# A transformer block with sparse and dense experts: reshaped gates, no end stage, U products beside the gates

## The chip, the cores and the metric

The kernel runs on one core of a Trainium2 chip. The metric is device time in microseconds (us), median of three runs. A profiled execution, taken separately, gives the rows below.

## The reference

One block over 1024 tokens of width 1024, float32. A mixing part (RMS norm, w_in, a pooling mixer and a gated mixer, w_out, residual) gives h. Then the PEER feed-forward, and a last RMS norm:

```python
q = (xb @ wq).reshape(T, 8, 2, 128)                   # 8 heads, 2 halves
s = einsum('thpd,phkd->thpk', q, keys)                # 16 lists of 128 scores
s_top, i_top = top_k(s, 16)
cand = s_top[:, :, 0, :, None] + s_top[:, :, 1, None, :]
best_s, best_pos = top_k(cand.reshape(T, 8, 256), 16) # 16 of 16384 experts per head
gate = softmax(best_s)
act = gelu(einsum('td,thkd->thk', xb, u_tab[idx]))
out = einsum('thk,thkd->td', gate * act, v_tab[idx])
```

## The kernel before

Tokens are eight blocks of 128. They pass the mixing part in three groups: first (blocks 0, 1), middle (2 to 5), last (6, 7). The feed-forward is done in two ways.

**Sparse blocks (0, 1, 6, 7).** For each of a token's 128 experts GpSimd (POOL) gathers one U row per token, 512 KB for a block of 128 tokens (`gather`, L475), and VectorE (DVE) takes the dot product (L501). `sparse_v` (L513) gathers V rows, four tokens at a time; ScalarE (ACT) sets the weights into a zero-padded tile `wz` (L520), and TensorE (PE) sums with 16 matmul instructions per step (L531), 32 steps per block. Parts are named U0, V0, U1 and so on; `sparse` (L665) hands them out in phases: EARLY before the dense loop, LATE beside it, with 32 rows (AFTER) kept back. `behind` (L487) ties the U0 and V0 matmuls to marks in PE's order.

**Dense blocks (2 to 5), 512 tokens.** All 16384 experts are computed. Expert (a, b) is row a of column b; there are 128 columns. First the gates are spread into a table G[expert, token] in DRAM (`gates_dense`, L554): for four tokens at a time (a step; TB = 4, 128 steps in all) DVE compares the token's 128 first and second keys with a row of numbers (`oh`, L567, L569), gate values are multiplied in by ACT for two tokens (L579) and by DVE for two (L581), PE multiplies the two one-hot sets (L582), and ACT copies the result from the accumulator to `gs` (two copies, L585); 32 tokens fill two half tiles, which go out (L589). `scale` (L592) normalises the middle group's rows, held in `sd`, into a high and a low part `xdh`, `xdl`. Then `dense` (L604): for every column c it loads U and V (L628, L633), splits both, computes U's product by 24 matmuls (`mu`, L642), gelu (L644), times the gates read from G (`gc`, L639; L645), splits that, and every three columns `down` (L615) multiplies by V (24 matmuls a column, `mm`, L619) and adds into `hD` (L623). `finish` (L545) does the last norm and the output.

**Selection.** `score` (L340) makes the lists' scores and calls `top16` (L368, five DVE operations) on each; `pick` (L380) selects 16 of the candidate sums for a block, `turn` (L462) transposes the result.

**Order.** Python generators set the trace order: `weave` (L695) takes so many steps of the gates per step of the last group's mixing, residual and score (L784 to L788); the rest of the gates follows (L798), then selection of blocks 6 and 7 (L800), scaling, EARLY, and the dense loop with LATE beside it (L817). A scheduler fills gaps on each engine with later instructions that are ready, so instructions can run ahead of this order. After the loop an end stage opens 16 row buffers (`rowe`) and does the last 32 rows of V7 (L822). Loads and stores are issued by SP's queue, gathers by POOL's.

Of the kernel before, what the change touches and what calls it, by code (L numbers as in the profile page):

```python
# [17 lines left out]
P = 128  # L18
# [8 lines left out]
PH = 8  # L27
# [20 lines left out]
GS = 3  # L48
# [18 lines left out]
def hybrid_block(ctx: ExitStack, tc: tile.TileContext, t: dict, out: bass.AP):  # L67
# [40 lines left out]
    gS = dram.tile([S, D], F32, name="gS")  # L108

# [193 lines left out]
    def residual(fc, fr, chunks, most):  # L303
# [6 lines left out]
        for q in range(4):  # L310
            cols = slice(q * WC, (q + 1) * WC)
            for ch, p in zip(chunks, project(fr, "w_out", q * WC, [ch.a for ch in chunks], True)):
                nc.vector.tensor_add(ch.h[:, :, cols], ch.h[:, :, cols], p)

                def quarter(ch=ch, q=q, cols=cols):
                    hg = tmp(fr, 2 * WC).rearrange("p (k e) -> p k e", e=WC)
                    nc.vector.tensor_mul(hg, ch.h[:, :, cols], g2row[:, None, cols].to_broadcast([P, NB, WC]))
                    if not d0 <= ch.t0 // P < d0 + DBLK:
                        nc.sync.dma_start(gS[ch.t0:ch.t0 + N, cols].rearrange("(k p) e -> p k e", p=P), hg)
# [4 lines left out]
                    nc.scalar.activation(ch.s[:, 2 * q:2 * q + 2, :], p, AF.Copy)  # L324
# [15 lines left out]
    def score(fr, tk, chunks):  # L340

        for ch in chunks:
            for k in range(NB):
# [15 lines left out]
        for q in range(NLIST // 2):  # L359
# [6 lines left out]
            yield  # L366

# [37 lines left out]
    def pick_heads(tk, top, tix, n, keys, gate_kh):  # L405
# [46 lines left out]
        for i in range(2):  # L452
            eq = tk.tile([P, TK, TK, PH], BF16, name="eq", tag="eq", bufs=1)[:, :, :, :n]
# [59 lines left out]
    def sparse_v(b):  # L513
# [4 lines left out]
        for j in range(32):  # L518
            z = wz[j % 2]
# [34 lines left out]
    def gates_dense(gp, b):  # L554
# [4 lines left out]
        for part in range(P // GT):  # L559
            kb = (b - d0) * (P // GT) + part  # L560
            gs = [gp.tile([P, NK // 2, GT], F32, name="gs", bufs=GS) for _ in range(2)]
            for t0 in range(0, GT, TB):

                oh = gp.tile([P, 2 * TB, NK], F32, name="oh", bufs=OH)
                tok = part * GT + t0
                half = TB // 2
                nc.vector.tensor_tensor(oh[:, 0:TB, :], iota_k[:, None, :].to_broadcast([P, TB, NK]),  # L567
                                        iT[:, 0, tok:tok + TB, None].to_broadcast([P, TB, NK]), op=ALU.is_equal)
                nc.vector.tensor_tensor(oh[:, TB:TB + half, :], iota_k[:, None, :].to_broadcast([P, half, NK]),  # L569
                                        iT[:, 1, tok:tok + half, None].to_broadcast([P, half, NK]), op=ALU.is_equal)  # L570
                if t0 // TB % 2:
                    p = ps1.tile([P, TB, NK], F32, name="mu", bufs=2)
                else:
                    p = ps.tile([P, TB, NK], F32, name="mm")
                for i in range(TB):
                    at = slice(tok + i, tok + i + 1)
                    c = oh[:, TB + i, :]
                    if i < half:
                        nc.scalar.activation(c, c, AF.Copy, scale=iT[:, 2, at])  # L579
                    else:  # L580
                        nc.vector.tensor_scalar(c, iota_k, iT[:, 1, at], iT[:, 2, at], op0=ALU.is_equal, op1=ALU.mult)  # L581
# [5 lines left out]
            for i, g in enumerate(gs):  # L587
                n = NK // GI // 2
                nc.sync.dma_start(G[i * n:(i + 1) * n, kb].rearrange("a i b t -> i a (b t)"),  # L589
                                  g.rearrange("i (a b) t -> i a (b t)", b=GI))  # L590

    def scale(tk, xdh, xdl):  # L592

        both = tk.tile([P, 2, ND], F32, name="both", tag="eq", bufs=1)
        r2B, x = both[:, 0, :], both[:, 1, :]
# [4 lines left out]
        for c in range(NDC):  # L600
            nc.vector.tensor_mul(x, sd[:, c, :], r2B)
            split(xdh[:, c, :], xdl[:, c, :], x)

    def dense(de, xdh, xdl):  # L604

        v_rows = t["peer_v"].rearrange("(a b) d -> b a d", b=NK)
        xd = [(xdh[:, c, :], xdl[:, c, :]) for c in range(NDC)]
        with tc.tile_pool(name="da", bufs=2, side="right", reuse_waits="tile") as da:
# [17 lines left out]
            for c in range(NK):  # L626
                raw = de.tile([P, NDC, P], F32, name="raw_u", tag="raw", bufs=3)
                nc.sync.dma_start(raw, t["uT"][c])  # L628
                uh = de.tile([P, NDC, P], F32R, name="uh")
                ul = de.tile([P, NDC, P], F32R, name="ul")  # L630
                split(uh, ul, raw)
# [9 lines left out]
                p = ps1.tile([P, ND], F32, name="mu", bufs=2)  # L641
                mm3(p, [(uh[:, i, :], ul[:, i, :]) for i in range(NDC)], xd)  # L642
                a = de.tile([P, ND], F32, name="a", bufs=2)
                nc.scalar.activation(a, p, AF.Gelu_apprx_tanh)  # L644
                nc.vector.tensor_mul(a.rearrange("i (k t) -> i k t", t=GT), a.rearrange("i (k t) -> i k t", t=GT), gc[:, :, c % GI, :])  # L645
                wh = da.tile([P, ND], F32R, name="wh", bufs=GROUP + 1)
# [3 lines left out]
                if c == 1:  # L650
                    load()
# [215 lines left out]
```

## Time and profile before

| what | us |
|---|---|
| median of 3 runs (lowest, highest) | 2702.26 (2700.18, 2703.74) |
| the profiled execution's own time | 2707.89 |
| its span, first to last instruction | 2705.8 |
| PE busy / DVE / ACT / POOL in the span | 2438.1 / 1896.4 / 774.3 / 1198.3 |
| moved by DMA | 831.49 MB, mean 307 GB/s |

Busy time is a union per engine. PE's matmuls overlap in a row's durations, so rates are read from their starts. PEld is PE's weight load. The granted clock (PEclk) is a share of full speed; PE has two levels, 1.2 and 2.4 GHz. A wait is put down to what ended it last.

### The profile page before, as it was taken

To read this page: it belongs to the slowest core of one execution; us is meant where nothing else is said; L and a number is where in the kernel's file an instruction comes from. 1 tells how busy PE (TensorE), PEld (TensorE's weight loads), DVE (VectorE), ACT (ScalarE), POOL (GpSimd) and SP (SyncE) were. 2 spreads that over 40 slices of the span, in tenths; PEclk is the share of its full clock that TensorE was granted. 3 is DMA by queue.
4 is the path that set the end of the run, shared out by engine and by line. 5 is a ranking of instruction groups with operands and counts; after the bars stand their busy time and mean duration, and the time that the engine had idled before them with its cause. 6 is when DMAs were issued, how large, how long until landed. Compare 5 with 4: busy or idle time off the path is not lost.

```text
span 2705.8 us, 34765 instructions
## 1 busy us (share of the span) xinstructions
PE 2438.1 (90%) x11968; PEld 1862.7 (69%) x11968; DVE 1896.4 (70%) x4643; ACT 774.3 (29%) x1424; POOL 1198.3 (44%) x1098
## 2 busy tenths in 40 slices
PE   7997899888866467999999999999999999999993
PEld 6886788767645144777777777777777777766770
DVE  2389979987797977986776767666676766433451
ACT  3220011245635252222222222322222222222220
POOL 0034753143443544655555555465455555344004
PEclk9998999999978689999999999999999999999996
DMA  7677998599988799999999999899999999889317
GB/s 250 210 245 230 384 344 284 168 313 315 333 286 296 255 307 348 361 356 324 365 354 342 341 339 364 328 361 375 327 342 359 349 348 331 324 329 359 119 39 287
DMA packets 345392, 831.49 MB, mean 307 GB/s; under 512 B 25216, under 2 KB 158848, under 8 KB 345216
## 3 DMA queue, kind: packets, MB, share of 16 engines
q0 software_dynamic: 147456, 536.94, 54.0%
q1 hardware_dynamic: 197760, 292.33, 31.4%
q8 instruction: 95, 1.56, 0.2%
q14 instruction: 81, 0.66, 0.1%
HBM read 785.13 MB, written 44.04 MB: 306 GB/s over the span
## 4 chain that ended last, share of the span: by engine, by line
PE 67%; DVE 15%; DMA 9%; issue 5%; ACT 2%; POOL 1%; SPq 0%; POOLq 0%; ACTq 0%; DVEq 0%
PE mm L176 8%; PE mm L139 8%; PE mm L140 8%; PE mu L141 8%; PE mm L141 8%; PE mu L139 8%; PE mu L140 8%; PE po L531 8%; DVE junk L501 3%; DMA G<-gs 2%; DMA rowt<-peer_v,idxT 2%; DVE rest L372 1%; PE mm L582 1%; DMA w<-w_out 1%; PE mu L582 1%
## 5 line engine op out<-in xcount | busy, mean ns | idle before, releaser
L480 POOL DMA_INDIRECT rowt<-peer_v,idxT x432 | 500.5, 1159 | 709.0 <-PE po L531 501.6
L480 POOL DMA_INDIRECT rowv<-peer_u,idx x288 | 353.6, 1228 | 176.4 <-DVE junk L501 105.7
L480 POOL DMA_INDIRECT rowt<-peer_u,idx x224 | 261.4, 1167 | 346.5 <-DVE top L370 166.4
L139 PE MATMUL mm<-vh,wh 128*128 128x512 f32 x1024 | 400.8, 395 | 14.4 <-ACT wh L131 8.4
L141 PE MATMUL mu<-xdh,ul 128*128 128x512 f32 x1024 | 403.0, 394 | 6.6 <-DVE ul L132 6.6
L139 PE MATMUL mu<-xdh,uh 128*128 128x512 f32 x1024 | 401.2, 393 | 6.2 <-ACT xdh L131 3.7
L140 PE MATMUL mu<-xdl,uh 128*128 128x512 f32 x1024 | 401.8, 392 | 1.2 <-DVE xdl L132 0.7
L140 PE MATMUL mm<-vl,wh 128*128 128x512 f32 x1024 | 401.0, 392 | 0.1
L501 DVE SCALAR_TENSOR_TENSOR junk<-rowv,h 128x1024 bf16<-128x1024 f32 x288 | 352.0, 1222 | 44.2 <-DMA rowv<-peer_u,idx 41.2
L141 PE MATMUL mm<-vh,wl 128*128 128x512 f32 x1024 | 376.9, 392 | 0.0
L623 DVE TENSOR_TENSOR hD<-hD,mm 128x512 f32<-128x512 f32 x344 | 225.8, 682 | 184.4 <-PE mm L141 183.5
L501 DVE SCALAR_TENSOR_TENSOR junk<-rowt,h 128x1024 bf16<-128x1024 f32 x224 | 271.9, 1214 | 19.6 <-DMA rowt<-peer_u,idx 18.2
L531 PE MATMUL po<-rowt,wz 128*32 128x512 f32 x1728 | 237.8, 650 | 38.0 <-DMA rowt<-peer_v,idxT 38.0
L139 PEld LDWEIGHTS mm<-vh,wh 128*128 128x128 f32 x1024 | 193.0, 189 | 75.1 <-issue 14.2
L141 PEld LDWEIGHTS mu<-xdh,ul 128*128 128x128 f32 x1024 | 192.6, 188 | 65.8 <-DVE ul L132 9.4
L139 PEld LDWEIGHTS mu<-xdh,uh 128*128 128x128 f32 x1024 | 192.1, 188 | 58.7 <-issue 9.2
L140 PEld LDWEIGHTS mu<-xdl,uh 128*128 128x128 f32 x1024 | 192.8, 188 | 53.8 <-issue 9.2
L141 PEld LDWEIGHTS mm<-vh,wl 128*128 128x128 f32 x1024 | 192.6, 189 | 50.1 <-issue 9.2
L140 PEld LDWEIGHTS mm<-vl,wh 128*128 128x128 f32 x1024 | 193.2, 189 | 42.4 <-issue 2.5
L644 ACT ACTIVATE a<-mu 128x512 f32<-128x512 f32 x128 | 76.0, 594 | 491.2 <-PE mu L141 490.0
L132 DVE SCALAR_TENSOR_TENSOR ul<-raw_u,uh 128x1024 fp32r<-128x1024 f32 x128 | 156.2, 1220 | 78.3 <-ACT uh L131 78.3
L131 ACT ACTIVATE vh<-raw_v 128x1024 fp32r<-128x1024 f32 x128 | 131.0, 1052 | 235.8 <-PE mm L141 216.9
(167 smaller groups left out, 3374.3 us busy)
## 6 DMA issues: line engine op xcount, KB each, us to landing
raw_u<-uT SPq DMA_DIRECT2D x128, 512.0 KB, 6.9
raw_v<-peer_v SPq DMA_DIRECT2D x128, 512.0 KB, 7.2
G<-gs SPq DMA_DIRECT2D x32, 1024.0 KB, 14.8
w<-wq SPq DMA_DIRECT2D x48, 512.0 KB, 6.6
w<-w_in SPq DMA_DIRECT2D x36, 512.0 KB, 4.8
w<-w_out SPq DMA_DIRECT2D x24, 512.0 KB, 6.6
h<-x SPq DMA_DIRECT2D x16, 512.0 KB, 7.7
rowt<-peer_v,idxT POOLq DMA_INDIRECT x432
```

Source lines behind the costliest of these rows:

```text
L131: nc.scalar.activation(hi, src, AF.Copy)
L132: nc.vector.scalar_tensor_tensor(lo, src, 1.0, f32(hi), op0=ALU.mult, op1=ALU.subtract)
L139: nc.tensor.matmul(dst, lh, rh, start=first and c == 0, stop=False)
L140: nc.tensor.matmul(dst, lh, rl, start=False, stop=False)
L141: nc.tensor.matmul(dst, ll, rh, start=False, stop=last and c == n - 1)
L176: mm = nc.tensor.matmul(dst[:, i, :], lhs, rhs, start=c == 0, stop=c == NDC - 1)
L480: ins = nc.gpsimd.indirect_dma_start(out=rowt, out_offset=None, in_=t[table], in_offset=bass.IndirectOffsetOnAxis(ap=ids, axis=0))
L501: nc.vector.scalar_tensor_tensor(junk, r, 1.0, h, op0=ALU.mult, op1=ALU.mult, accum_out=act[:, j:j + 1])
L531: mm = nc.tensor.matmul(po[g * 32:(g + 1) * 32, q * HALF:(q + 1) * HALF], z[:, g, 31 - j:63 - j], r[:, q * HALF:(q + 1) * HALF], start=j = ...
L582: mm = nc.tensor.matmul(p[:, i, :], oh[:, i, :], c, start=True, stop=True)
L623: nc.vector.tensor_add(hq, hq, p)
L644: nc.scalar.activation(a, p, AF.Gelu_apprx_tanh)
```

## The change

The gate step compares both keys of four tokens in one operation, ACT alone multiplies the gate values in, the matmuls of one step write interleaved (token innermost), and one copy empties the accumulator into one tile of 128 rows. The middle group's rows go to DRAM (`sS`) instead of `sd`; `scale` reads them back, two chunks at a time, and stands ahead of the rest of the gates. The U products of the first AHEAD = 7 columns (`up`) are handed out over the last 46 gate steps and kept in `ua`. The last group's scores go to DRAM (`cS`); `lists` reads them and makes the top-16 lists behind the gates, just ahead of the selection of blocks 6 and 7. V0 is split: 64 rows EARLY, 64 LATE. The loop hands out all 768 LATE rows by column 125, in proportion to U and V products done; the end stage is gone. Until seven columns are done the loop's gathers use the old row buffers alone. Four `wz` tiles take the place of two; `wh` and `wl` have three buffers instead of four, `sc` three instead of four; the final norm's row loads inside the loop.

```diff
-ROWS, VROWS, EROWS = 7, 4, 16
+AHEAD = 7
+ROWS, VROWS = 7, 4
-EARLY = ({"U0": 128}, {"V0": 128, "U1": 64})
-LATE = ({"U1": 64}, {"V1": 128, "U6": 128}, {"V6": 128, "U7": 128}, {"V7": 128})
-AFTER = 32
+EARLY = ({"U0": 128}, {"V0": 64, "U1": 64})
+LATE = ({"V0": 64, "U1": 64}, {"V1": 128, "U6": 128}, {"V6": 128, "U7": 128}, {"V7": 128})
...
-    for i in range(2):
+    for i in range(4):
         z = const.tile([P, 4, 63], F32, name=f"wz{i}")
...
-                    nc.scalar.activation(ch.s[:, 2 * q:2 * q + 2, :], p, AF.Copy)
+                    sq = ch.s[:, 2 * q:2 * q + 2, :]
+                    nc.scalar.activation(sq, p, AF.Copy)
+                    if D0 <= ch.t0 < D0 + ND:
+                        nc.sync.dma_start(sS[2 * q:2 * q + 2, :, ch.t0 - D0:ch.t0 - D0 + N]
+                                          .rearrange("c p s -> p c s"), sq)
...
-                sc = tk.tile([P, 2, NK], F32, name="sc", bufs=4)
+                sc = tk.tile([P, 2, NK], F32, name="sc", bufs=3)
                 nc.scalar.activation(sc, pk[:, k], AF.Copy, scale=ch.r2[:, k:k + 1])
+                if by:
+                    nc.sync.dma_start(cS[b - LAST[0] // P, q], sc)
+                    continue
...
+    def lists(tk, b):
+        found[b] = lists_of(tk, 4)
+        top, tix = found[b]
+        for q in range(NLIST // 2):
+            sc = tk.tile([P, 2, NK], F32, name="sc", bufs=3)
+            nc.sync.dma_start(sc, cS[b - LAST[0] // P, q])
+            for e in range(2):
+                top16(tk, top[:, 2 * q + e, :], tix[:, 2 * q + e, :], sc[:, e, :], NK)
...
-            gs = [gp.tile([P, NK // 2, GT], F32, name="gs", bufs=GS) for _ in range(2)]
+            gs = gp.tile([P, NK, GT], F32, name="gs", bufs=2)
...
-                nc.vector.tensor_tensor(oh[:, 0:TB, :], iota_k[:, None, :].to_broadcast([P, TB, NK]),
-                                        iT[:, 0, tok:tok + TB, None].to_broadcast([P, TB, NK]), op=ALU.is_equal)
-                nc.vector.tensor_tensor(oh[:, TB:TB + half, :], iota_k[:, None, :].to_broadcast([P, half, NK]),
-                                        iT[:, 1, tok:tok + half, None].to_broadcast([P, half, NK]), op=ALU.is_equal)
+                nc.vector.tensor_tensor(oh, iota_k[:, None, None, :].to_broadcast([P, 2, TB, NK]),
+                                        iT[:, 0:2, tok:tok + TB, None].to_broadcast([P, 2, TB, NK]), op=ALU.is_equal)
...
-                    mm = nc.tensor.matmul(p[:, i, :], oh[:, i, :], c, start=True, stop=True)
+                    c = oh[:, 1, i, :]
+                    nc.scalar.activation(c, c, AF.Copy, scale=iT[:, 2, tok + i:tok + i + 1])
+                    mm = nc.tensor.matmul(p[:, :, i], oh[:, 0, i, :], c, start=True, stop=True)
                 marks.append(mm.ins)
-                for g, cols in zip(gs, (slice(0, NK // 2), slice(NK // 2, NK))):
-                    nc.scalar.activation(g[:, :, t0:t0 + TB].rearrange("p k i -> p i k"), p[:, :, cols], AF.Copy)
+                nc.scalar.activation(gs[:, :, t0:t0 + TB], p, AF.Copy)
...
+        for c in range(0, NDC, 2):
+            x = de.tile([P, 2, ND], F32, name="raw_x", tag="raw", bufs=3)
+            nc.sync.dma_start(x, sS[c:c + 2].rearrange("c p s -> p c s"))
+            nc.vector.tensor_mul(x, x, r2B[:, None, :].to_broadcast([P, 2, ND]))
+            split(xdh[:, c:c + 2, :], xdl[:, c:c + 2, :], x)
+
+    def up(de, c, a, xd):
+        raw = de.tile([P, NDC, P], F32, name="raw_u", tag="raw", bufs=3)
+        nc.sync.dma_start(raw, t["uT"][c])
+        uh = de.tile([P, NDC, P], F32R, name="uh")
+        ul = de.tile([P, NDC, P], F32R, name="ul")
+        split(uh, ul, raw)
+        p = ps1.tile([P, ND], F32, name="mu", bufs=2)
+        mm3(p, [(uh[:, i, :], ul[:, i, :]) for i in range(NDC)], xd)
+        nc.scalar.activation(a, p, AF.Gelu_apprx_tanh)
+        return a
...
+                a = ahead[c] if c < AHEAD else up(de, c, de.tile([P, ND], F32, name="a", bufs=2), xd)
...
-    for _ in gates:
-        pass
+    scale(de, xdh, xdl)
+    def ups():
+        for c in range(AHEAD):
+            ahead.append(up(de, c, ua.tile([P, ND], F32, name="ua"), xd))
+            yield
+    left = DBLK * steps - DBLK * steps * 2 // 3 - 8
+    weave(gates, left, (ups(), 0, AHEAD, left))
     for b in (6, 7):
+        lists(tk, b)
         for _ in pick(tk, b):
             pass
         turn(b)
...
-        while done * NK < (c + 1) * (steps - AFTER):
+        if c + 1 == AHEAD:
+            uas.close()
+            gav = opened(gavs, name="gav", bufs=VROWS, reuse_waits="tile")
+            beside += [(gav, "rowv", VROWS), (gat, "rowt", ROWS)]
+        while done * work < min(2 * (c + 1) - min(c + 1, AHEAD), work) * steps:
             next(gathered, None)
             done += 1
-    with tc.tile_pool(name="gae", bufs=EROWS, side="right", reuse_waits="tile") as gae:
-        beside[:] = [(gae, "rowe", EROWS)]
-        homes["U"] = homes["V"] = beside[:]
-        for _ in gathered:
-            pass
```

## Rows read from the trace of the kernel before

**Rows 1.** Stages: window and length, busy us (instructions) of PE, PEld, DVE, ACT, POOL; clock, DMA, GB/s

```profile
559.00:1013.00 454.00, 318.97 (x1885) 232.27 (x1883) 368.82 (x1255) 224.34 (x578) 196.17 (x171) 0.83 0.88 300
1013.00:1106.00 93.00, 72.50 (x276) 51.02 (x275) 75.22 (x123) 26.59 (x37) 49.23 (x38) 0.93 0.97 354
1106.00:2300.00 1194.00, 1186.16 (x5644) 891.47 (x5644) 856.90 (x1243) 322.58 (x454) 658.08 (x546) 1.00 0.95 347
2508.00:2640.00 132.00, 127.72 (x578) 103.03 (x576) 66.41 (x111) 37.96 (x52) 0.00 (x0) 1.00 0.24 79
2640.00:2706.00 66.00, 23.38 (x128) 5.59 (x128) 8.69 (x35) 2.41 (x8) 29.96 (x32) 0.69 0.74 289
```

**Rows 2.** The chain that ended last, at its end: start, us, what

```profile
2642.81 2.64 DMA out<-hD
...
2684.72 7.92 DMA rowe<-peer_v,idxT
```

**Rows 3.** Timeline of PE in the dense loop: start, us, engine, line, operation

```profile
2509.91 1.94 PE L531 MATMUL po<-rowt,wz 128*32 128x512 f32 x16
2511.78 0.50 PE L139 MATMUL mm<-vh,wh 128*128 128x512 f32 x1
...
2621.66 0.39 PE L139 MATMUL mu<-xdh,uh 128*128 128x512 f32 x1
...
2623.93 0.39 PE L140 MATMUL mu<-xdl,uh 128*128 128x512 f32 x1
```

**Rows 4.** Groups of instructions, whole run: count, busy us, mean ns, idle before

```profile
L501 DVE SCALAR_TENSOR_TENSOR junk<-rowv,h 128x1024 bf16<-128x1024 f32 x288 | 352.0, 1222 | 44.2 <-DMA rowv<-peer_u,idx 41.2
...
L645 DVE TENSOR_TENSOR a<-a,gc 128x512 f32<-128x512 f32 x128 | 88.0, 688 | 139.5 <-ACT a L644 135.4 <-DMA gc<-G 4.1
...
L324 ACT ACTIVATE sd<-mm 128x512 f32<-128x512 f32 x8 | 4.5, 595 | 60.4 <-PE mm L323 60.4
...
L210 ACT ACTIVATE rB<-mm 128x256 f32<-128x256 f32 x4 | 1.4, 386 | 0.0
```

**Rows 5.** The same groups from 559 to 1013 us, the gates stage

```profile
L567 DVE TENSOR_TENSOR oh<-iota_k,iT 128x512 f32<-128x512 f32 x128 | 87.3, 682 | 43.3 <-PE mm L582 32.2 <-PE mu L582 10.9
L582 PE MATMUL mm<-oh 128*128 128x128 f32 x512 | 86.8, 316 | 36.4 <-ACT oh L579 36.4
L579 ACT ACTIVATE oh<-oh,iT 128x128 f32<-128x128 f32 x256 | 85.3, 387 | 36.0 <-DVE oh L569 35.5
L531 PE MATMUL po<-rowt,wz 128*32 128x512 f32 x452 | 81.9, 799 | 38.0 <-DMA rowt<-peer_v,idxT 38.0
L581 DVE TENSOR_SCALAR oh<-iota_k,iT 128x128 f32<-128x128 f32 x256 | 77.2, 340 | 0.0
...
L585 ACT ACTIVATE gs<-mm 128x256 f32<-128x256 f32 x128 | 71.8, 633 | 66.4 <-PE mm L582 33.4 <-DMA G<-gs 32.4
...
L569 DVE TENSOR_TENSOR oh<-iota_k,iT 128x256 f32<-128x256 f32 x128 | 53.3, 416 | 0.0
```

**Rows 6.** Timeline of DVE, one gate step and the start of the next

```profile
996.29 0.68 DVE L567 TENSOR_TENSOR oh<-iota_k,iT 128x512 f32<-128x512 f32 x1
...
997.74 0.68 DVE L567 TENSOR_TENSOR oh<-iota_k,iT 128x512 f32<-128x512 f32 x1
```

**Rows 7.** Groups, whole run: one of the five operations of a top-16 list

```profile
L371 DVE FIND_INDEX8 tix<-top,sc 128x8 uint32<-128x128 f32 x128 | 36.0, 283 | 0.0
```

**Rows 8.** Stages of 20 us while DVE selects, columns as in rows 1

```profile
880.00:900.00 20.00, 5.09 (x25) 1.07 (x21) 20.00 (x122) 0.83 (x3) 5.86 (x6) 0.59 0.90 328
900.00:920.00 20.00, 6.36 (x30) 1.26 (x22) 20.00 (x85) 0.73 (x3) 11.39 (x9) 0.50 0.56 183
```

**Rows 9.** The chain, in the middle group's residual step

```profile
277.10 19.26 DMA w<-w_out
```

**Rows 10.** The chain, between the gates and the dense loop

```profile
1028.64 17.84 DMA gc<-G
```

**Rows 11.** The chain, eight gate matmuls in a row

```profile
566.40 1.09 PE mm L582 x8
```

More of the change, by code (lines that the diff above doesn't have):

```diff
@@ L338, in residual, with score @@
                 r2s[ch.t0 // P + k] = ch.r2[:, k:k + 1]
-    def score(fr, tk, chunks):
+    def score(fr, tk, chunks, by=False):
         for ch in chunks:
-            for k in range(NB):
+            for k in range(0 if by else NB):
                 found[ch.t0 // P + k] = lists_of(tk, 4)
@@ L571, in gates_dense @@
                 if t0 // TB % 2:
-                    p = ps1.tile([P, TB, NK], F32, name="mu", bufs=2)
+                    p = ps1.tile([P, NK, TB], F32, name="mu", bufs=2)
                 else:
-                    p = ps.tile([P, TB, NK], F32, name="mm")
+                    p = ps.tile([P, NK, TB], F32, name="mm")
                 for i in range(TB):
[L576 to L581, printed above, removed]
@@ L586, in gates_dense @@
                 yield
[L587 to L595, printed above, removed]
+            nc.sync.dma_start(G[:, kb].rearrange("a i b t -> i a (b t)"),
+                              gs.rearrange("i (a b) t -> i a (b t)", b=GI))
@@ L596, in scale @@
+    def scale(de, xdh, xdl):
+        r2B = de.tile([P, ND], F32, name="r2B", tag="a", bufs=2)
         p = ps.tile([P, HALF], F32, name="mm")[:, :ND]
@@ L599, in scale, with dense @@
         nc.scalar.activation(r2B, p, AF.Copy)
[L600 to L604, printed above, removed]
+        for c in range(0, NDC, 2):
[13 more added lines that the diff above has]
+        return a
+    def dense(de, xd, ahead):
         v_rows = t["peer_v"].rearrange("(a b) d -> b a d", b=NK)
-        xd = [(xdh[:, c, :], xdl[:, c, :]) for c in range(NDC)]
         with tc.tile_pool(name="da", bufs=2, side="right", reuse_waits="tile") as da:
@@ L651, in dense @@
                     load()
+                    fgrow.append(da.tile([P, D], F32, name="fgrow", bufs=1))
+                    nc.sync.dma_start(fgrow[0], rows(t["final_g"], D))
                 if len(grp) == GROUP:
@@ L669, in sparse @@
             n = max(phase.values())
-            if beside:
-                kinds = {name[0] for name in phase}
-                homes["U"] = beside[:1] if len(kinds) > 1 else beside
-                homes["V"] = beside[1:] if len(kinds) > 1 else beside
+            kinds = {name[0] for name in phase}
             for i in range(n):
+                if beside:
+                    homes["U"] = beside[:1] if len(kinds) > 1 else beside
+                    homes["V"] = beside[1:] if len(kinds) > 1 else beside
                 for name, m in phase.items():
@@ L748, in hybrid_block @@
     first = group(FIRST, ma[1:])
-    middle = group(MIDDLE, [sd[:, :, i * N:(i + 1) * N] for i in range(len(MIDDLE))])
     last = group(LAST, ma[1:])
@@ L753, in hybrid_block @@
     fc = opened(fcs, name="fc", bufs=1, side="right")
+    middle = group(MIDDLE, [fc.tile([P, NDC, N], F32, name=f"s{i}") for i in range(len(MIDDLE))])
     later.append(lambda: stats(0, NB))
@@ L783, in hybrid_block @@
         next(gates, None)
-    lasts = chain(mix(fc, fr, last, 1), residual(fc, fr, last, 1), score(fr, tk, last))
+    lasts = chain(mix(fc, fr, last, 1), residual(fc, fr, last, 1), score(fr, tk, last, True))
     for _ in range(TURN + 1):
@@ L795, in hybrid_block @@
     xdl = xd.tile([P, NDC, ND], F32R, name="xdl")
-    fgrow.append(de.tile([P, D], F32, name="fgrow", bufs=1))
-    nc.sync.dma_start(fgrow[0], rows(t["final_g"], D))
-    for _ in gates:
-        pass
+    scale(de, xdh, xdl)
+    xd = [(xdh[:, c, :], xdl[:, c, :]) for c in range(NDC)]
+    uas = ExitStack()
+    ua = opened(uas, name="ua", bufs=AHEAD, reuse_waits="tile")
+    ahead = []
+    def ups():
[4 more added lines that the diff above has]
+    weave(gates, left, (ups(), 0, AHEAD, left))
     for b in (6, 7):
+        lists(tk, b)
         for _ in pick(tk, b):
@@ L803, in hybrid_block @@
         turn(b)
-    scale(tk, xdh, xdl)
     gps.close()
```

34 lines of the change are left out of this document (12 added, 22 removed).

## The prediction

> **What bounds the kernel now.** I read the busy time by stage first [rows 1]. From 559 to 1013 us, the gates stage, no engine is full: VectorE (DVE) is busy 369 of 454 us, TensorE (PE) 319 at 0.83 of full clock, ScalarE (ACT) 224. From 1106 to 2300 us, the dense loop with the gathers beside it, PE is busy 1186 of 1194 us at full clock and the DMA engines 95% at 347 GB/s. So PE is the bound there and DMA stands just under it. From 2508 to 2640 us the loop runs with no gather at all (POOL 0, DMA 24%). From 2640 us the end stage follows: PE 23 of 66 us. The chain of work that ended last [rows 2] shows what fills it: the dense rows leave at 2642.8 to 2645.5, and only then come gathers, waits for them and V products, up to the last row's output at 2705.8.
>
> **Prices on PE.** In the dense loop ten matmuls start in 2.27 us [rows 3], so 0.227 us each; a column has 24 for U and 24 for V-down. One step of a V block (four rows, 16 matmuls) takes 1.87 us there [rows 3].
>
> **The change, part by part.** The sum is made against the profiled span of 2705.8 us.
>
> (1) *No end stage.* The last finish is now that of the dense rows, whose output lands at 2645.5 in the chain; the 60 us behind it go: **-60**. The eight steps of V7 that lay there go into the loop: 8 x 1.87 = **+15**.
>
> (2) *U products of 7 columns beside the gates.* 7 x 24 x 0.227 = **-38** of PE in the loop. Beside the gates they find PE 135 us idle [rows 1]. Their casts and splits go with them: 7 DVE operations of 1.22 us [rows 4], little beside 369. Price without that cover: the same 38 us back.
>
> (3) *V0 split in two.* Its 16 later steps go into the loop: 16 x 1.87 = **+30**. They leave the gates stage, where PE waited 38 us for V rows in all [rows 5]; their gathers stand on POOL's queue between U1's, as before.
>
> So the loop's PE work is 15 - 38 + 30 = **+7**: (128 + 121) x 24 x 0.227 + 112 x 1.87 = 1566 against 1559 us. The loop ran from 1015 to 2640, so 66 us of it were start and stalls (1013 to 1106 has PE busy 73 of 93 us [rows 1]), which I keep.
>
> (4) *Reshaped gates.* Per step of four tokens DVE had four operations, 682 + 416 + 2 x 340 ns [rows 5], that follow each other in 1.45 us (996.29 to 997.74) [rows 6]; now one compare of 1024 elements. The trace has no such compare; a two-input operation of that size takes 1.22 us [rows 4], about 1.14 from start to start: -0.31 x 128 = -40. ACT had 2 x 387 + 2 x 633 = 2.04 us; now 4 x 387 and one copy of 512 elements. That copy lies between 595 ns [rows 4] and twice the old one, 1266: ACT gains or loses +13 to +99 us in a stage where it is idle 230. So it hides, unless the stage falls under about 340 us. The PE part is a rival below. The 32 stores of G become 16 of twice the size, with two whole buffers instead of one and a half: ACT waited 32 us for such stores [rows 5]; I take nothing, bounds -32 and +32.
>
> (5) *Selection moved past the gates.* 32 top-16 lists (blocks 6 and 7) leave the score step: five operations like the 283 ns shown [rows 7], at most 1.6 us each with what lies between, 52 us in sum. The two selections stood behind the gates in the code already, but DVE ran selections while gates waited: from 880 to 920 us DVE is busy 40 of 40 us, PE 11, and ACT runs six operations in all [rows 8]. On the way are 16 stores and 16 loads of 128 KB, and each store stands in SP's queue behind an ACT result, with the next weights behind it.
>
> What (3) to (5) leave of the gates stage: if everything stays inside, DVE's 369 - 40 + 17 (scale and splits) = 346 at the same 81% gives 427, so -27. If lists and selections go past, DVE falls to some 255, PE (319 - 30 + 38 = 327) and ACT become the floor, and the stage could end near 345: -110. But then up to 100 us of DVE work comes back behind it. I take **-50**, near the first, since the work only moves; ends 0 and -110.
>
> (6) *What DMA adds in the loop.* It now carries 768 gathers instead of 672, and 121 U columns: 121 x 0.524 + 128 x 0.786 + 768 x 0.524 = 567 MB instead of 520. At the 347 GB/s of [rows 1] that is 1634 us, against PE's 1566 plus 66. Two resources full together must wait for each other at times: **+20**, bounds 0 (95% busy was no limit) and +80 (see the rival).
>
> (7) *Scores kept in DRAM.* The middle group's normalised rows are stored by 8 DMAs of 256 KB in its residual step, on SP's queue between the w_out loads, for which PE waited 19 us once [rows 9]; four loads come back. **+5**, bounds 0 and +19.
>
> At nothing: four zero-padded weight tiles instead of two (ACT waits for the V step before last, a wait that can only shrink); three score buffers instead of four (ACT copies them straight out); wh and wl with three buffers instead of four, as vh and vl have now, covered by the next columns' U products, without which a group would wait for gelu, gate product, cast and split, four operations like the 0.69 us of [rows 4], 42 times; the final norm's row, loaded later.
>
> Sum: -60 + 7 - 50 + 20 + 5 = **-78**, 2628 of span. The profiled execution took 2707.9 us, 5.6 over the median of 2702.3; the same -78 on the median gives **2624 us**.
>
> **Where the stall goes.** After the last gate, G has to go out and come back: the read alone took 17.8 us [rows 10]. Before, the first columns' U products ran meanwhile, at the pace of the scaling. Now these are done, and PE waits for G, for V0's late rows and for DVE.
>
> **Rivals.**
>
> *DMA becomes the loop's bound.* For: 95% over 1194 us [rows 1]. Against: short stretches moved 354 GB/s [rows 1], and no V step waits for its rows in the loop. With 1634 us plus about 55 in which it can't be full (G's way at the start, three columns behind the last gather) the loop takes 1690 instead of 1652: +38, **2662 us**. Chance 0.2.
>
> *Matmuls that write with a stride cost more.* The gates' 1024 matmul instructions now write every fourth element of a bank. In the trace all matmuls write dense rows; the nearest row is ACT's copy that writes at a stride, 633 ns [rows 5] for 256 elements, against 386 dense [rows 4], 1.64 times. Taken onto 0.136 us per instruction (eight in 1.09 us [rows 11]) that is 0.087 x 1024 = 89 us on PE, 416 busy in the stage in place of 327. The 50 us won in the gates would be gone: **2674 us**. Against it: these fp32 matmuls pass only one column per 0.83 ns, half the rate of the dense loop's (512 in 0.227 us). Chance 0.15. The Trainium skill ("PSUM — Partial Sum Buffer", Specifications) speaks for this rival: it says that the memory works in 8-byte lines and that a non-contiguous access pattern slows matmuls significantly. By that rule the time would be this rival's; no run here shows it yet.
>
> *The U products don't run beside the gates.* Their tiles lie where the last group's weights lay, and they share two PSUM buffers (mu) with every second gate step. If they come behind the gates, (2) gives nothing: 2624 + 38 = **2662 us**. Against: the code hands them out over the last 46 gate steps, which lie behind the last group's work. Chance 0.08.
>
> *Slower: selection between gates and loop.* If lists and selections stand on DVE behind the last gate as the code has them, the first columns' splits, gate products and sums queue behind them in DVE's order and PE waits for those: 52 us of lists and two selections of 20 to 40 us [rows 8], 92 to 132. The gates gain nothing else, if gathers and G's stores pace them (DMA is 88% busy there [rows 1]): 2702.3 - 60 + 7 + 20 + 5 + 92 = 2766, less up to 40 for the lighter compare: **2726 to 2766 us**. It decides where the time PE loses there is over 78 us more than the gates win. Against it: DVE had 85 us idle in the stage before and gets 40 more, and the old selections already slipped into such gaps. Chance 0.12.
>
> **How the numbers follow.** Forecast 0.45, the rivals 0.2, 0.15, 0.08 and 0.12. The likeliest case's own range is 2565 to 2660 (gates -110 to -20, with (6) at 0 to 40). The range that should hold 8 in 10 goes on over the three faster rivals with their upper ends: 2560 to 2700; outside are the slower one and the tail below. A measurement of this kernel can tell about 0.2% from no change, 5.4 us. Slower by more: 0.12. Within it, the far ends of the DMA and stride cases: 0.05. Faster: 0.83.
>
> **What will show it.** Right: no V rows gathered after the dense rows' output; POOL busy to within some 40 us of the end; gates that end 30 to 80 us sooner; U products of seven columns among the gate matmuls; one compare of about 1.2 us per step. Stride: a mean of the gate matmuls well over 316 ns at full clock. DMA bound: V steps in the loop that wait for their rows, DMA over 97%. Selection: DVE full of lists and selections behind the last gate, and PE idle for more than 80 us before the first down product. I am wrong altogether if PE in the loop shows over 100 us idle.

## The result, and the profile after

The changed kernel takes 2726.93 us (median of 4 runs, 2720.48 to 2731.63), the kernel before beside it 2701.22: ratio 1.0093, 95% interval 1.007 to 1.0117. It is **slower by 0.9%**, a small change but clear of the interval, where 2624 us were forecast. The profiled execution has a span of 2725.4 us against 2705.8.

The parts that were meant to win did win. First the busy time by stage after (window and length, then PE, PEld, DVE, ACT, POOL, clock, DMA, GB/s as in [rows 1]):

```profile
940.00:990.00 50.00, 28.65 (x164) 15.43 (x162) 43.75 (x179) 14.38 (x35) 23.20 (x18) 0.75 1.01 349
990.00:1100.00 110.00, 109.08 (x488) 76.96 (x482) 67.93 (x96) 26.85 (x37) 54.09 (x47) 0.97 0.92 330
1100.00:2300.00 1200.00, 1116.15 (x5194) 811.36 (x5193) 810.39 (x1203) 289.01 (x423) 673.26 (x567) 0.98 0.94 345
2520.00:2725.00 205.00, 182.16 (x780) 144.53 (x772) 99.28 (x174) 51.33 (x70) 0.00 (x0) 0.95 0.27 90
```

The last copy of a gate step starts at 950.38 us; before, it started at 1012.57. The first down products come at about 991, and from there PE is full (109 of 110 us), where [rows 1] had 73 of 93. GpSimd gathers nothing after 2520: the end stage is gone. But in the loop from 1100 to 2300 PE is now idle 84 of 1200 us, against 8 of 1194 in [rows 1]. In the last 205 us, with no gather and DMA at 27%, it is idle 23; 12 of these belong to the finish behind the last V product, which ends at 2713. So most of the loss lies where gathers run beside the loop.

The gates stage by groups, 540 to 990 us (busy us, mean ns of one, idle before), answers to [rows 5]:

```profile
L594 ACT ACTIVATE oh<-oh,iT 128x128 f32<-128x128 f32 x512 | 161.2, 394 | 37.3 <-DVE oh L586 36.8
L586 DVE TENSOR_TENSOR oh<-iota_k,iT 128x1024 f32<-128x1024 f32 x128 | 153.0, 1219 | 33.9 <-PE mm L595 18.8 <-PE mu L595 14.7
L595 PE MATMUL mm<-oh 128*128 128x128 f32 x512 | 81.7, 302 | 32.5 <-ACT oh L594 32.3
L595 PE MATMUL mu<-oh 128*128 128x128 f32 x512 | 78.6, 296 | 10.4 <-ACT oh L594 10.4
L597 ACT ACTIVATE gs<-mm 128x512 f32<-128x512 f32 x64 | 37.7, 589 | 16.3 <-PE mm L595 15.8
```

The compare takes 1219 ns, the accumulator copy 589, and the matmuls that write at a stride 302 and 296 ns, no more than the 316 of [rows 5]. These means mix both clock levels; the median of one matmul is 275 ns before and after.

What ends PE's idle time in the loop, 1106 to 2300 us (the groups of PE), shows where the time went; two groups of the kernel before stand below for the same stretch:

```profile
L142 PE MATMUL mm<-vh,wh 128*128 128x512 f32 x680 | 276.7, 412 | 42.9 <-ACT wh L134 38.6 <-DVE hD L645 3.9
L144 PE MATMUL mu<-xdh,ul 128*128 128x512 f32 x679 | 270.2, 398 | 17.6 <-DVE ul L135 17.6
L142 PE MATMUL mu<-xdh,uh 128*128 128x512 f32 x680 | 270.1, 397 | 21.3 <-ACT uh L134 21.3
...
L141 PE MATMUL mu<-xdh,ul 128*128 128x512 f32 x772 | 303.7, 393 | 4.8 <-DVE ul L132 4.8
L139 PE MATMUL mm<-vh,wh 128*128 128x512 f32 x768 | 299.4, 393 | 3.0 <-DVE hD L623 1.5 <-ACT wh L131 1.3
```

PE waits for U's cast and split (`uh`, `ul`), and for the cast `wh`, which comes from U's product by way of gelu and gates. Before, it was 4.8 us in all on `ul` and 1.3 on `wh`. One such place in the timeline, one engine after another (start, us, engine, line, operation, in brackets the idle time before it and what ended it; SPq is SP's queue):

```profile
1201.83 0.33 SPq L650 DMA_DIRECT2D raw_v<-peer_v  x1
1208.69 0.38 SPq L650 DMA_DIRECT2D raw_v<-peer_v  x1
1222.97 0.33 SPq L650 DMA_DIRECT2D raw_v<-peer_v  x1
...
1238.29 2.94 ACT L134 ACTIVATE vh<-raw_v 128x1024 fp32r<-128x1024 f32 x3
...
1242.13 2.36 DVE L135 SCALAR_TENSOR_TENSOR vl<-raw_v,vh 128x1024 fp32r<-128x1024 f32 x2
1245.54 1.23 DVE L135 SCALAR_TENSOR_TENSOR vl<-raw_v,vh 128x1024 fp32r<-128x1024 f32 x1
1254.52 1.23 DVE L521 SCALAR_TENSOR_TENSOR junk<-rowv,h 128x1024 bf16<-128x1024 f32 x1 [1.41 <-DMA rowv<-peer_u,idx]
1255.67 1.22 DVE L135 SCALAR_TENSOR_TENSOR ul<-raw_u,uh 128x1024 fp32r<-128x1024 f32 x1
...
1243.38 0.33 SPq L618 DMA_DIRECT2D raw_u<-uT  x1
1244.51 0.33 SPq L650 DMA_DIRECT2D raw_v<-peer_v  x1
1246.80 0.33 SPq L618 DMA_DIRECT2D raw_u<-uT  x1
...
1251.07 1.06 ACT L134 ACTIVATE uh<-raw_u 128x1024 fp32r<-128x1024 f32 x1 [3.04 <-DMA raw_u<-uT]
1256.21 1.06 ACT L134 ACTIVATE uh<-raw_u 128x1024 fp32r<-128x1024 f32 x1 [4.08 <-DMA raw_u<-uT]
...
1252.18 0.50 PE L142 MATMUL mu<-xdh,uh 128*128 128x512 f32 x1 [1.09 <-ACT uh L134]
1256.95 0.80 PE L144 MATMUL mu<-xdh,ul 128*128 128x512 f32 x1 [4.03 <-DVE ul L135]
1257.54 0.63 PE L142 MATMUL mu<-xdh,uh 128*128 128x512 f32 x1
1257.96 0.63 PE L143 MATMUL mu<-xdl,uh 128*128 128x512 f32 x1
...
1262.21 0.39 PE L144 MATMUL mu<-xdh,ul 128*128 128x512 f32 x1
1262.44 0.39 PE L142 MATMUL mu<-xdh,uh 128*128 128x512 f32 x1
```

Read it from the top. Three V loads go out one after another (the U loads between them are split before 1223). Their three casts come together at 1238.29. The first V split ends at about 1243.35, and SP issues a U load at 1243.38; the third ends at 1246.77 (1245.54 + 1.23), and SP issues the next U load at 1246.80. ACT casts that one 9.4 us later, at 1256.21, as soon as it has landed. PE, out of work, waits 1.09 us for the cast of the first of these U loads and then 4.03 us for its split. That split is late for a second reason: DVE has a dot product of gathered rows ahead of it, which itself waits 1.41 us for its rows. Then PE's matmuls start 0.42 us apart instead of 0.23 until 1262, at the lower of the two clock levels (last section).

Why does a U load wait for a split of V? Both loads share three slots (tag `raw`), and a slot comes free when what it holds has been split. The diff does one thing that the prediction did not read. Before, a column loaded U first and V second. Now `up` stands behind the load and split of V, so a column's V takes a slot ahead of its U. SP's own waits (total, times, longest) show it for the U load, L618 after (1100 to 2300 us) and L628 before (1106 to 2300):

```profile
SPq L618 <- DVE vl L135: 246.6, 54, 20.4
SPq L618 <- DVE ul L135: 160.9, 25, 13.2
...
SPq L628 <- DVE ul L132: 243.8, 29, 12.3
SPq L628 <- DVE vl L132: 119.0, 57, 10.3
```

U's load waits 247 us for V's splits, where it waited 119. The slots are not taken strictly in turns, since U loads follow U's splits too. The timelines of SP and DVE, with a slot counted as held from the start of its load to the end of its split, show what is new: between 1100 and 2300 us three V's hold all three slots 17 times, 127 us in all, and the next U load can't go out. In the kernel before that never happens.

V's split is late because `vh` has three buffers, which come back only as a group's down products end: ACT's casts to `vh` waited 79.0 us for those in this stretch. Before, they waited 148.1 us (1106 to 2300) and PE did not feel it, so this wait by itself does not stall PE.

### The profile page after: what moved, and what is told of

Read it like the earlier page. It is cut to its first block, busy times and chain, and to the rows that moved or that the text cites. A ratio compares the mean times of both kernels' runs of the same rounds, so it can differ in the third digit from the quotient of the medians.

```text
span 2725.4 us, 34387 instructions
## 1 busy us (share of the span) xinstructions
PE 2458.2 (90%) x11968; PEld 1869.3 (69%) x11968; DVE 1857.0 (68%) x4251; ACT 794.0 (29%) x1552; POOL 1221.4 (45%) x1100
## 4 chain that ended last, share of the span: by engine, by line
PE 61%; DVE 16%; DMA 12%; issue 5%; ACT 4%; POOL 2%; SPq 0%; DVEq 0%; POOLq 0%; ACTq 0%
PE mm L142 8%; PE po L551 8%; PE mm L143 7%; PE mu L142 7%; PE mu L144 7%; PE mu L143 7%; PE mm L144 7%; PE mm L179 7%; DVE junk L521 3%; DMA rowv<-peer_u,idx 3%; DMA rowt<-peer_v,idxT 2%; DMA rowt<-peer_u,idx 2%; DMA raw_u<-uT 2%; DVE rest L392 1%; DVE oh L586 1%
## 5 line engine op out<-in xcount | busy, mean ns | idle before, releaser
L500 POOL DMA_INDIRECT rowt<-peer_v,idxT x448 | 529.2, 1181 | 497.4 <-PE po L551 357.5
L500 POOL DMA_INDIRECT rowv<-peer_u,idx x309 | 380.1, 1230 | 208.9 <-DVE junk L521 127.7
L142 PE MATMUL mm<-vh,wh 128*128 128x512 f32 x1024 | 412.0, 411 | 44.3 <-ACT wh L134 39.8
L521 DVE SCALAR_TENSOR_TENSOR junk<-rowv,h 128x1024 bf16<-128x1024 f32 x309 | 377.8, 1223 | 108.7 <-DMA rowv<-peer_u,idx 104.0
L500 POOL DMA_INDIRECT rowt<-peer_u,idx x203 | 242.7, 1195 | 455.8 <-DVE top L390 166.3
L143 PE MATMUL mm<-vl,wh 128*128 128x512 f32 x1024 | 414.0, 404 | 2.5 <-DVE vl L135 2.5
L144 PE MATMUL mm<-vh,wl 128*128 128x512 f32 x1024 | 368.6, 398 | 1.3 <-DVE wl L135 1.3
L521 DVE SCALAR_TENSOR_TENSOR junk<-rowt,h 128x1024 bf16<-128x1024 f32 x203 | 247.1, 1217 | 19.0 <-DMA rowt<-peer_u,idx 17.7
L143 PEld LDWEIGHTS mm<-vl,wh 128*128 128x128 f32 x1024 | 199.5, 195 | 49.7 <-DVE vl L135 4.9
L659 DVE TENSOR_TENSOR a<-a,gc 128x512 f32<-128x512 f32 x121 | 83.7, 692 | 174.4 <-ACT a L624 174.3
```

Of the source, the lines that this page charges most:

```text
L142: nc.tensor.matmul(dst, lh, rh, start=first and c == 0, stop=False)
L143: nc.tensor.matmul(dst, lh, rl, start=False, stop=False)
L144: nc.tensor.matmul(dst, ll, rh, start=False, stop=last and c == n - 1)
L500: ins = nc.gpsimd.indirect_dma_start(out=rowt, out_offset=None, in_=t[table], in_offset=bass.IndirectOffsetOnAxis(ap=ids, axis=0))
L521: nc.vector.scalar_tensor_tensor(junk, r, 1.0, h, op0=ALU.mult, op1=ALU.mult, accum_out=act[:, j:j + 1])
```

## The experiments

The theories. **DMA**: the loop carries 47 MB more (the prediction's rival). **Buffers**: `wh` and `wl` with three buffers instead of four. **Order**: V ahead of U in a column; its rival **pace**: 768 gathers by column 125 crowd the loop, whatever the order. Times of before differ by batch (2701 to 2709 us), so the ratios tell.

### Less DMA, and the wh buffers

Gathers of half the bytes (the rows' second halves are not fetched, the first half stands in for both):

```diff
-        ins = nc.gpsimd.indirect_dma_start(out=rowt, out_offset=None, in_=t[table],
+        ins = nc.gpsimd.indirect_dma_start(out=rowt[:, :HALF], out_offset=None, in_=t[table].rearrange("n (q e) -> (n q) e", q=2),
```

> The changed kernel with gathers of half the bytes: each row brings 512 of its 1024 numbers and the products use them twice, so that every engine does the same work (the output is not the reference's). Theory D: TensorE's idle time in the loop goes and the time is 2610 to 2650 us. Theory W: the waits for wh stay over 100 us and the time is 2680 to 2730 us.

2856.16 us, ratio 1.0567 (1.0522 to 1.0611). Its loop:

```profile
1100.00:2200.00 1100.00, 976.96 (x4630) 665.11 (x4629) 717.59 (x1093) 237.51 (x373) 758.96 (x639) 0.94 0.75 239
```

DMA falls to 75%, and PE is idle more (123 of 1100 us), so a full DMA is not what PE waits for. The gathers end at 2248, some 260 us sooner than in the changed kernel, and U's load waits 479.0 us for V's splits between 1100 and 2300 us, against 246.6: the same wait has grown. Why was not pursued.

Four buffers for `wh` and `wl` again (three `wz` tiles make the room), and three in the kernel before:

```diff
-                wh = da.tile([P, ND], F32R, name="wh", bufs=GROUP)
-                wl = da.tile([P, ND], F32R, name="wl", bufs=GROUP)
+                wh = da.tile([P, ND], F32R, name="wh", bufs=GROUP + 1)
+                wl = da.tile([P, ND], F32R, name="wl", bufs=GROUP + 1)
```

> The changed kernel with four buffers for wh and wl again (and three zero-padded weight tiles, so that it fits). Theory W, the third buffer was needed: ScalarE's 179 us of waits for the down products, ahead of its casts of wh, go; the loop shrinks by 60 to 100 us and the time is 2630 to 2670 us. Theory D, the loop is bound by DMA: ScalarE still waits over 100 us for the U columns, and the time stays at 2700 to 2730 us.

> The kernel before with three buffers for wh and wl, nothing else. Theory W: the loop gets 60 to 100 us longer, 2760 to 2800 us, with over 100 us of ScalarE waits for the down products. Theory D: no change within 10 us, 2690 to 2712 us, since the gathers per column are the same.

2711.47 us, ratio 1.0016 (0.9999 to 1.0034), so by the ratios about 21 us below the changed kernel, with PE still idle 80 of 1200 us; and 2708.12, ratio 1.001 (0.9989 to 1.0031), no change. The buffers are a small part of it.

### The gates alone, the end alone

The reshaped gates in the kernel before (compare, scaling, matmul and accumulator layout; the copies go into the old half tiles), and the kernel before with no row kept back:

```diff
-                    mm = nc.tensor.matmul(p[:, i, :], oh[:, i, :], c, start=True, stop=True)
+                    mm = nc.tensor.matmul(p[:, :, i], oh[:, 0, i, :], c, start=True, stop=True)
...
-AFTER = 32
+AFTER = 0
```

> The kernel before with the reshaped gates alone (one compare, all gate values by ScalarE, interleaved matmul output, dense copies, but into the two half tiles of before). The prediction's terms: gates 30 to 60 us shorter with the gate matmuls' mean at 300 to 320 ns, 2650 to 2680 us. Rival, the strided write costs: mean of the gate matmuls over 400 ns, 2700 us or more.

> The kernel before, with the 32 rows that it keeps back handed out in the loop (AFTER = 0), so that the end stage does nothing: the change's first part alone. Theory 'order': 2701 - 60 + 15 = 2656, with 10 for late rows at the end 2650 to 2675 us. Rival 'pace': the loop takes back most of it, 2690 to 2715 us, with PE idle in the loop up by 30 us or more.

Gates: 2680.76 us, ratio 0.9902 (0.9868 to 0.9936), about 27 us won, just under the 30 to 60 expected; PE's gate matmuls mean 306 ns. End: 2659.88 us, ratio 0.9831 (0.9805 to 0.9856), 45 us won, as part (1) says (-60 + 15; the interval allows 39 to 53), and PE busy 1187 of 1194 us in the loop. That speaks against "pace" but does not settle it: this kernel's late parts are 704 rows by the last column, the changed kernel's 768 by column 125.

### U first, V first

In the changed kernel the line of `up` goes ahead of V's load; in the kernel before, U's load and split go behind V's:

```diff
+                a = ahead[c] if c < AHEAD else up(de, c, de.tile([P, ND], F32, name="a", bufs=2), xd)
                 raw = de.tile([P, D], F32, name="raw_v", tag="raw", bufs=3)
...
-                a = ahead[c] if c < AHEAD else up(de, c, de.tile([P, ND], F32, name="a", bufs=2), xd)
```

> The changed kernel, with each column's U product (load, split, matmuls, gelu) written ahead of the load and split of its V rows again, as in the kernel before; all else as changed. Theory 'order': V's casts need vh and vl buffers that only the down products of the group before give back, and with V written first ACT's queue holds U's cast, and SP's the next U load, behind that wait; PE then runs dry once per group of three columns. With U first the loop's PE idle falls from about 85 of 1200 us to under 30 and the time from 2727 to 2630 to 2665 us. Rival 'pace' (768 gathers handed out by column 125 crowd the loop, whatever the order inside a column): idle stays over 60 of 1200 us and the time between 2705 and 2735.

> The kernel before, with each column's V load and split written ahead of its U load and split, and nothing else of the change. Theory 'order': stalls as in the changed kernel, 1.5 to 2.5 us in each of 42 groups, so 2701 + 60 to 100 = 2765 to 2805 us, PE idle in the 1200 us from the loop's start on over 60. Rival 'pace': within 10 us of 2705, idle as before, 8 of 1194.

**2616.85 us**, ratio 0.9677 (0.9653 to 0.9702), and **2822.09 us**, ratio 1.0422 (1.0374 to 1.047). The one line takes the changed kernel from 0.9% slower to 3.2% faster, and the same swap costs the kernel before 118 us. The stages of U first, one in the loop and one near its end:

```profile
1100.00:2300.00 1200.00, 1197.03 (x5682) 897.44 (x5681) 851.06 (x1240) 321.28 (x460) 635.33 (x536) 1.00 0.93 343
2560.00:2580.00 20.00, 10.90 (x68) 4.45 (x70) 1.91 (x3) 0.42 (x2) 10.24 (x11) 0.76 0.92 343
```

and of V first in the kernel before, the loop and two groups of PE in it:

```profile
1106.00:2300.00 1194.00, 1135.90 (x5402) 823.04 (x5403) 815.58 (x1200) 296.55 (x435) 682.54 (x582) 0.99 0.96 356
...
L139 PE MATMUL mm<-vh,wh 128*128 128x512 f32 x700 | 281.2, 404 | 30.1 <-ACT wh L131 25.2 <-DVE hD L623 4.0
L141 PE MATMUL mu<-xdh,ul 128*128 128x512 f32 x705 | 280.3, 398 | 16.5 <-DVE ul L132 16.5
```

With U first 3 of 1200 us are idle; with V first 58 of 1194, on the same casts and splits as in the changed kernel. "Pace" falls: U first hands out the same 768 rows by column 125, with the same bytes, and doesn't stall. The sign of "order" holds in both; both effects are larger than expected (2617 lies below 2630 to 2665, and 118 us above 60 to 100).

The idle time is not the whole loss. From the first V product to the last, in the changed kernel and with U first, then in the kernel before and with V first in it:

```profile
991.00:2713.00 1722.00, 1625.11 (x7611) 1183.88 (x7611) 1052.60 (x1537) 419.98 (x612) 830.72 (x714) 0.98 0.86 315
990.00:2562.50 1572.50, 1568.34 (x7515) 1163.63 (x7515) 1042.47 (x1507) 413.46 (x600) 813.12 (x701) 1.00 0.92 339
...
1048.00:2635.80 1587.80, 1568.98 (x7483) 1179.09 (x7483) 1054.05 (x1526) 426.04 (x607) 777.17 (x655) 1.00 0.88 324
1052.60:2745.80 1693.20, 1607.72 (x7507) 1187.63 (x7507) 1050.91 (x1518) 422.84 (x607) 760.53 (x651) 0.99 0.82 303
```

Each order that stalls also has PE busy longer, 57 and 39 us, for nearly the same number of matmuls, at a lower mean clock (0.98 and 0.99 against 1.00). In the changed kernel the dense products gain 150 us by U first, the time only 110: the last V product now ends at 2562.5, but the last gather is issued at 2584.14.

How V first stalls the kernel before is shown only as far as these waits. Three V's hold all slots there for 27 us between 1100 and 2300, as with U first (27).

### Which part of the order: loads or casts

Only U's load ahead of V's, the rest V first; and only V's load first, U's whole product ahead of V's cast:

```diff
...
+                ru = None if c < AHEAD else uload(de, c)
                 raw = de.tile([P, D], F32, name="raw_v", tag="raw", bufs=3)
                 nc.sync.dma_start(raw, v_rows[c])
...
```

> The changed kernel with only U's load written ahead of V's load; the casts, splits and products stay V first. If SP's queue is what makes U late (its load issued behind V's, and held for a slot of the three shared load buffers), this gives most of the 110 us of the run with U first: 2615 to 2650. If the order of the casts on ScalarE is (U's cast behind a V cast that waits for a buffer of vh), it gives little: 2700 to 2730, with PE idle in 1100 to 2300 us still over 50.

> The changed kernel with only V's load written first; U's load, cast, split, product and gelu stand ahead of V's cast and split. The counterpart: by the order of the casts 2615 to 2650 us with PE idle under 30 in 1100 to 2300; by SP's queue 2700 to 2730.

2614.29 us (ratio 0.97, 0.9653 to 0.9746) and 2727.09 (1.0111, 1.0066 to 1.0156). One loop row and one SP wait of each, U's load first and then V's:

```profile
1100.00:2300.00 1200.00, 1197.97 (x5688) 898.43 (x5687) 852.41 (x1242) 322.02 (x461) 635.82 (x537) 1.00 0.93 344
...
SPq L618 <- DVE vl L135: 133.0, 59, 14.4
```

```profile
1100.00:2300.00 1200.00, 1116.67 (x5225) 809.66 (x5227) 812.62 (x1207) 291.30 (x427) 668.13 (x569) 0.98 0.94 346
...
SPq L618 <- DVE vl L135: 237.1, 53, 20.3
```

The order of the loads decides it; three V's hold all slots for 25 us in the first run and for 125 in the second. The half of theory "order" that put ACT's queue to blame falls: writing the casts in another order moves nothing.

### The slot and the vh buffer

Two ways to cut the link with the order left as changed: a fourth slot for the loads, or a fourth buffer for `vh` and `vl`. Both are paid for with row buffers of the gathers, so two controls have five row buffers alone, in the changed kernel and with U first:

```diff
-    raw = de.tile(..., tag="raw", bufs=3)
+    raw = de.tile(..., tag="raw", bufs=4)
...
-ROWS, VROWS = 7, 4
+ROWS, VROWS = 6, 4
...
-                vh = da.tile([P, D], F32R, name="vh", bufs=GROUP)
+                vh = da.tile([P, D], F32R, name="vh", bufs=GROUP + 1)
...
-ROWS, VROWS = 7, 4
+ROWS, VROWS = 5, 4
```

> The changed kernel, order as changed, with four slots instead of three for the loads that U and V share, and six row buffers instead of seven to make the room. If the slot is the link (U's load of column c+1 takes the slot that V of column c gives back only when split), U's load then waits for the split of V one column earlier, as with U first: PE's idle in 1100 to 2300 us falls from 84 to under 25, and the time to 2615 to 2670 (the lost row buffer may cost some). If U is late because it stands behind V in SP's queue for another reason, idle stays over 50 and the time 2710 to 2740.

> The changed kernel, order as changed, with four buffers for vh and vl instead of three; five row buffers instead of seven for the gathers make the room. If the wait for vh's release by the down products is what holds U's cast, the wait of the vh cast for PE falls to under a third of 100 us over the run, PE's idle by half or more, and the time to 2640 to 2690 (the fewer row buffers may cost some of it). If the order alone makes U late, whatever the buffers, 2715 to 2740.

> The changed kernel with five row buffers instead of seven and nothing else: the control for the run with four vh buffers (2706 us). If the two row buffers cost what that run did not win, the stalls stay (PE idle over 60 in 1100 to 2300) and the time is well over 2727: 2760 to 2810. If row buffers are free, 2720 to 2735, and then the vh buffer itself wins only 20.

> U first, as in the run of 2617 us, with five row buffers instead of seven. If the gathers become the bound as soon as the loop runs without stalls, the time rises to 2685 to 2715, like the runs with a fourth vh buffer or load slot, and GpSimd gathers until some 20 us from the end while the dense loop ends near 2560 to 2570. If row buffers cost nothing here either, 2610 to 2630, and what those two runs lack has another cause.

| kernel | us | ratio (95%) | PE idle, 1100 to 2300 | last V product ends, us | last gather, us |
|---|---|---|---|---|---|
| four slots, six rows | 2685.14 | 0.994 (0.9905 to 0.9975) | 5 | 2580.9 | 2658.89 |
| four vh, five rows | 2706.40 | 1.0024 (1.0003 to 1.0045) | 3 | 2565.9 | 2673.54 |
| five rows | 2698.03 | 0.9986 (0.9969 to 1.0004) | 47 | 2673.8 | 2670.91 |
| U first, five rows | 2698.69 | 0.9978 (0.9958 to 0.9997) | 3 | 2572.1 | 2668.59 |

The loop and the end with four slots:

```profile
1100.00:2300.00 1200.00, 1195.22 (x5648) 898.44 (x5648) 841.99 (x1227) 318.36 (x455) 635.84 (x523) 1.00 0.93 338
2600.00:2688.00 88.00, 30.17 (x160) 7.79 (x160) 13.36 (x66) 7.02 (x17) 33.31 (x36) 0.61 0.71 254
```

and U first with five row buffers:

```profile
1100.00:2300.00 1200.00, 1197.15 (x5702) 899.92 (x5701) 839.77 (x1223) 318.17 (x458) 645.30 (x531) 1.00 0.93 341
2600.00:2697.00 97.00, 32.31 (x192) 7.96 (x192) 13.37 (x66) 7.43 (x18) 38.39 (x41) 0.71 0.74 265
```

Either cut ends the stalls, and five row buffers alone, the control, leave 47 us of them (six alone were not tried). So the chain has both links: vh's release holds V's split, the split holds the slot, the slot holds U's load. (With four vh buffers V's cast still waits 145 us for PE in this stretch, where less than a third of 100 had been expected; PE does not feel it, as in the kernel before with its 148.) The times missed what was expected, because the row buffers count as soon as the loop runs freely. With five of them and U first the dense products are done at about 2572, but gathers go on to 2669 and an end of 97 us with PE a third busy is back; that costs 82 us. They also start the dense loop later (first V product at 1007.5 instead of 990). In the stalled loop five row buffers cost nothing, where 30 to 80 us more had been expected, and were even 29 us faster (PE idle 47 instead of 84). Why fewer row buffers ease the stalls stays open; three V's hold all slots even longer there, 170 us, so that state alone does not measure a stall.

### The covered U products, and the best version

U first with AHEAD = 1 instead of 7; and U first with four `wh` buffers:

> U first as in the run of 2617 us, with one column's U product beside the gates instead of seven: the change's second part all but undone. If the covered products are worth what the sum says, six columns x 24 x 0.227 = 33 us come back: 2640 to 2655. If the loop has slack elsewhere (G's way, the late V rows), nearer 2620 to 2635.

> U first as in the run above, and wh and wl with four buffers as before (three zero-padded weight tiles instead of four, for the room). Theory 'order': 5 to 25 us below the run with U first alone, near 2635. Rival 'pace': no more than the 0.8% that four buffers gave alone, so 2705 to 2715.

2622.19 us (0.9709, 0.9663 to 0.9755): in the whole time six covered products are worth 5 us (9 by the ratios), not 33, and even that lies within the intervals. The last gather is issued at 2591.22 instead of 2584.14. The last V product ends at 2605.9 instead of 2562.5: for PE's dense work the covered products are worth 43 us, but with U first and AHEAD = 7 the gathers set the end and hide it. (With AHEAD = 1 the loop's own row buffers also open six columns sooner.)

And **2598.99 us** (0.9614, 0.9589 to 0.9639), which beats both kernels, by 3.9% and 4.7%. Its gain over U first lies in the gathers: the last is issued at 2566.05 instead of 2584.14, while the dense products end 6 us later. Whether the `wh` buffers or the third `wz` tile in place of the fourth do that was not separated.

## Why the prediction was wrong

The prediction starts the loop where the gates end and forecasts a start at 970 and a length of 1652 us. Measured, the gates end at 951, earlier than that, and the loop runs to 2720, the span less the 5.5 us behind it. Counted in the same way it takes 1768 us, 116 more. From 951 to the last V product at 2713 PE is idle 118 us: 21 up to the first V product, 97 from there on, at a mean clock of 0.97.

- **The step that failed** is the sentence "66 us of it were start and stalls ..., which I keep". The stalls were kept because the loop's order was taken as kept. Part (2) read `up` as seven products moved out and overlooked that, for the other 121 columns, the diff moves U's load behind V's in SP's queue and in the three shared slots. What showed in its place: U's load waits 247 us for V's splits instead of 119, and PE is idle 84 of 1200 us instead of 8 of 1194. Putting U's load back ahead of V's, and nothing else, takes 113 us off (106 by the ratios).
- **(1) No end stage**: right, -45 by itself.
- **(2) U products beside the gates**: they do run there (3 x 56 matmuls of `mu`, 22 to 23 us busy for each of the three lines), and with U first six of them bring the last V product 43 us forward, 33 reckoned. The step from there to the time failed: the gathers then set the end, and the time gains 5.
- **(3) V0 split, (7) scores in DRAM**: not tried alone.
- **(4) and (5) Gates**: the mechanism was right. -27 for the shape alone; with lists and selections moved, the last gate comes 62 us sooner, the first V product 56 (991.83 against 1047.98). From 940 to 990 DVE is busy 44 of 50 us, mostly with selection, and PE 29.
- **(6) DMA**: +20 was not needed; with U first PE is busy 1197 of 1200 us at 343 GB/s.
- **"At nothing", wh and wl**: the fourth buffers are worth about 21 us in the changed kernel, 17 to 18 with U first, and nothing in the old loop. The cover named there, the next U products, does come late in the changed kernel, but with U first it holds (PE idle 3 of 1200 us), so it does not explain that gain.
- **Rivals.** The stride cost is not there: the median of a gate matmul is 275 ns before and after, its mean 302 and 296 ns against 316. At full granted clock these matmuls mostly start 0.112 us apart in both kernels, or 0.875 ns a column; the prediction's 0.136 us and 0.83 ns are slightly off. The Trainium skill ("PSUM — Partial Sum Buffer", Specifications) says that a non-contiguous access pattern slows matmuls significantly; for these fp32 matmuls of 128 columns, each writing every fourth element, the trace does not agree. The DMA rival fell with the half gathers and with U first. The slower rival had the sign, not the mechanism: PE lost 21 us between gates and loop, under the 78 at which it decides.
- The text did say what would mean "wrong altogether": over 100 us of PE idle in the loop. It is 118 from the end of the gates on.
- U first gives 2617 us, 7 below the forecast. That is partly luck: the gates gave 12 us more than forecast, the 20 of (6) were not needed, and most of (2) did not reach the time.

## What to carry to other kernels

Where two loads share a few slots, the order in which they are written decides which of them can hold the slots while the other, needed sooner, waits. When a diff turns inline code into a helper, check for each queue and each set of shared buffers what the call now stands behind. And when a stall is cut, ask what sets the end next: here the gathers and their row buffers, which had cost nothing in the stalled loop.

## What was not expected of the hardware

Two stretches of the changed kernel on either side of the idle times shown above (columns as in [rows 1]; the granted clock is the third number from the end):

```profile
1248.00:1252.00 4.00, 3.01 (x12) 2.18 (x12) 0.81 (x2) 0.96 (x2) 3.09 (x4) 1.00 0.99 391
1257.00:1262.00 5.00, 5.00 (x12) 3.98 (x13) 2.17 (x3) 0.26 (x1) 2.77 (x2) 0.50 1.03 410
```

The granted clock is 1.00 before (2.4 GHz) and 0.50 after (1.2 GHz). After PE had been idle 1.09 and 4.03 us, with little work between, its matmuls started 0.42 us apart instead of 0.23, eleven times: this stall cost some 2.2 us more than its length (an estimate, 11 x 0.2). ACT's accumulator copy of 128x256 that writes runs of four neighbouring elements takes 382 to 384 ns in the kernel with the gates alone, against 633 in [rows 5] for the same size and target in the old layout, with the read order changed too; which of the two sides cost the time was not separated.
